# A planner's release time for tiles under an adding transfer, and its wait between small vector instructions, in a two-layer decoder kernel

## The chip, the cores and the metric

The kernel runs on one core of a Trainium2 chip. Its metric is the device time of one execution in microseconds (us). The engines are TensorE (PE, with its weight loads as PEld), VectorE (DVE), ScalarE (ACT), GpSimd (POOL) and SyncE (SP, which here only issues transfers).

## What is computed

The reference is a trunk of two layers on 512 tokens of width 1024, in 32-bit floats:

```python
# per layer (DEPTH = 2, SEQ = 512, D_MODEL = 1024, D_FF = 4096)
xn = rms_norm(h, g_mix);  proj = xn @ w_in
att = dsa_attention(...)        # 8 heads; an indexer keeps the top 128 keys of each query
hm  = sigmoid(m_o) * rms_norm(mlstm_chunkwise(...))      # 4 heads of 128
h = h + concat([att, hm]) @ w_out
u = rms_norm(h, g_mlp) @ w_ff1
h = h + square(relu(u)) @ w_ff2
gate = sigmoid(rms_norm(h, g_ple) @ w_ple_gate + b)
h = h + gate * (p_i @ w_ple)
```

## The kernel before, in words

Every large product is made of three passes over operands split in two: a weight tile `raw` of 128 x 1024 floats comes from memory, ACT writes `hi`, its rounded form, and `lo` holds the rest; the product is hi*hi + hi*lo + lo*hi. There are two ways to get `lo` (`weight`, L521). In the plain way DVE subtracts `hi` from `raw`. In the other ("adder") ACT writes the negative of the rounded form into `lo`, and a transfer issued by POOL adds `raw` to it in place (L533, L534); so `raw` is read by that transfer until it lands. 126 of 212 weight tiles go this way: those of the values, the convolution's projections, the output projection, the second product of the MLP (ff2), and some of the first (ff1) and of the gate.

The rest of ff1 goes by a Strassen scheme (`left` L762, `pair` L792). A pair takes two weight tiles, r1 and r2, and makes sums of their quarters on DVE in `at` and in place; ACT and DVE then split these. In the MLP of a layer seven rounds run; each has two pairs and eight blocks of ff2 (four adder tiles).

Nothing runs in the order in which the program is written. The whole kernel is first recorded as a list of operations with their tiles. `Plan.schedule` (L248) then plays them through by a list of assumed costs: each engine takes the ready operation of highest rank whose new tiles have free places (rank: the longest path to the end, plus an urgency of its label, L51). Places are few: 3 for `raw`, 4 for `hi`, 4 for `lo` (L1341), handed out in the order in which they came free. The order in which each engine took its operations is then its program; the chip keeps it strictly. On the chip true dependencies and reuse of places are guarded by semaphores, so that the planner's times decide order and places, and nothing else.

Three assumed times matter here. `cost` gives a vector instruction on four columns 69 + 4 x 1.042 ns = 73 ns (L229). `lag` (L232) says how long after an operation's end its readers may start: 110 ns from DVE to DVE, and 5,500 ns after an adder was issued. A tile's place comes free `HOP` = 200 ns after the end of the operation that finishes last among its users (L356 to L360); an adder ends, for this purpose, 1,100 ns after POOL takes it.

Chains of small vector instructions stand where a root is taken: `rsqrt` (L545) is ten dependent instructions on tiles of 4 to 16 columns (rooms `tiny` and `wide`), and `spread` (L610) follows with a copy, a difference and two wide products, which TensorE needs to spread the roots over partitions. Between the two stand the first blocks of ff1 in the MLP. `norm`, their label, has an urgency of 180, well above the MLP's 0. On TensorE the matmuls of `mlp` are chained in program order (L189), the spread's two among them.

Of the kernel before, what the change touches and what calls it, by code (L numbers as in the profile page):

```python
# [55 lines left out]
class View:  # L56


    def __init__(self, buf, steps, index, p):
        self.buf, self.steps, self.index, self.p = buf, steps, index, p  # L60
# [66 lines left out]
class Plan:  # L127
# [5 lines left out]
    ENGINES = ("vector", "scalar", "gpsimd", "tensor", "sync")  # L133
    HOP = 200.0

    def __init__(self, rooms, caps):
        self.ops, self.rooms, self.caps = [], rooms, caps
        for e in self.ENGINES:
            setattr(self, e, Engine(self, e))
        self.chain, self.tail, self.hold = None, {}, None  # L140
        self.bufs = 0
        self.label, self.stage, self.bias = None, 0, 0
# [88 lines left out]
    @staticmethod  # L231
    def lag(a, b):  # L232

        if a == "adder":
            return 5500.0
        if a == b:
            return {"vector": 110.0, "scalar": 60.0, "gpsimd": 100.0}.get(a, 0.0)
        if b == "sync":
            return 1220.0
        if a == "sync":  # L240
            return 2200.0
        return 320.0 if b == "tensor" else 200.0 if a == "tensor" else 150.0
# [5 lines left out]
    def schedule(self):  # L248
        ops = self.ops
        for op in ops:  # L250
            for a in op.after:
                ops[a].before.append(op.n)
        for op in reversed(ops):
            c = min(self.cost(f) for f in op.forms)
            op.rank = c + max((ops[b].rank + self.lag(self.source(op), ops[b].forms[0][0]) for b in op.before),
                              default=0.0)
            op.left, op.ready, op.start = len(op.after), 0.0, None
        for op in ops:
            op.rank += 1000.0 * (URGENT.get(op.label, 0) + op.bias) - 1e7 * op.stage
        free = {k: list(range(n)) for k, n in self.rooms.items()}  # L260
        held = dict.fromkeys(self.caps, 0)
        queues = {e: {} for e in self.ENGINES}
        busy = dict.fromkeys(self.ENGINES, False)
        events, now, done = [], 0.0, 0
        live = {}
        idle = [-1e9, 0.0]

        def push(op):
            key = tuple(sorted(b.kind for b in op.new))
            for e in {f[0] for f in op.forms}:  # L270
                heapq.heappush(queues[e].setdefault(key, []), (-op.rank, op.n))

        def fits(op, relaxed=False):
            need = {}
            for b in op.new:
                need[b.room] = need.get(b.room, 0) + 1
            for k, n in need.items():
                if k not in free:
                    continue
                if len(free[k]) < n + (0 if relaxed else (MARGIN.get(op.label, MARGIN["s"]) if k == "s" else MARGIN.get(op.new[0].kind, 0))):  # L280
                    return False
            for b in op.new:
                for group, (kinds, cap) in self.caps.items():
                    if b.kind in kinds and held[group] >= cap:
                        return False
            return True

        for op in ops:
            if not op.left:
                push(op)  # L290
        order = []
        while done < len(ops):
            moved, relaxed = True, False
            while moved or not (events or relaxed):
                relaxed = not moved
                moved = False
                for e in self.ENGINES:
                    if busy[e]:
                        continue
                    best = None  # L300
                    for key, q in queues[e].items():
                        while q and ops[q[0][1]].start is not None:
                            heapq.heappop(q)
                        if q and (best is None or q[0] < best[0]):
                            op = ops[q[0][1]]
                            if fits(op, relaxed):
                                best = (q[0], q)
                    if best is None:
                        continue
                    op = ops[heapq.heappop(best[1])[1]]  # L310
                    op.form = next(f for f in op.forms if f[0] == e)
                    op.start = op.begin = now
                    for b in op.new:
                        live[b.name] = (b, op.label, round(now / 1000))
                        if b.room in free:
                            b.place = free[b.room].pop(0)
                        for group, (kinds, cap) in self.caps.items():
                            if b.kind in kinds:
                                held[group] += 1
                    busy[e] = True  # L320
                    order.append(op)
                    op.end = now + self.cost(op.form)
                    if e == "sync" and not now:
                        op.end += 900.0
                    if e == "tensor":
                        if now - idle[0] > 3300.0:
                            idle[1] = now + 3600.0
                        if now < idle[1]:
                            op.end += self.cost(op.form)
                        idle[0] = op.end  # L330
                    heapq.heappush(events, (op.end, 0, op.n, e))
                    moved = True
                    if relaxed:
                        break
            if not events:
                stuck = [(o.n, o.label, [b.kind for b in o.new]) for e in self.ENGINES for q in queues[e].values()
                         for _, i in q[:3] for o in (ops[i],) if o.start is None]
                self.live = live
                self.stuck = []
                raise RuntimeError(f"no place: {done} of {len(ops)} {stuck[:20]} { {k: len(v) for k, v in free.items()} } {held}")  # L340
            now, what, n, e = heapq.heappop(events)
            op = ops[n]
            if what == 0:
                busy[e] = False
                done += 1
                for b in op.before:
                    o = ops[b]
                    o.ready = max(o.ready, now + self.lag("adder" if op.form[:2] == ("gpsimd", "dma_start") else e,
                                                          o.forms[0][0]))
                    o.left -= 1  # L350
                    if not o.left:
                        if o.ready <= now:
                            push(o)
                        else:
                            heapq.heappush(events, (o.ready, 1, o.n, None))
                for b in {id(v.buf): v.buf for v in op.reads + op.writes}.values():  # L356
                    b.users -= 1
                    if not b.users:
                        heapq.heappush(events, (now + self.HOP, 2, n, b.name))
                        self.gone[b.name] = b  # L360
            elif what == 1:
                push(op)
            else:
                b = self.gone.pop(e)
                live.pop(b.name)
                if b.room in free:
                    free[b.room].append(b.place)
                for group, (kinds, cap) in self.caps.items():
                    if b.kind in kinds:
                        held[group] -= 1  # L370
        self.order, self.span = order, now
# [1055 lines left out]
```

## Time and profile before

| | us |
|---|---|
| median of 3 runs | 1380.51 (1380.43 to 1382.61) |
| profiled execution | 1384.69 |
| its span, first to last instruction | 1383.0 |
| PE busy | 1322.4 (96%) |
| DVE busy | 922.1 (67%) |
| ACT busy | 791.1 (57%) |

The stages of the profiled execution, by its windows: layer 1 has its mixing part to about 240 us, the way into the MLP to 300, the MLP to about 620, the gate to about 665; layer 2 the same from there, with the way into the MLP from 920 to 980 and the MLP to about 1310. All instructions have one line, L390, since the plan issues them in one place; so they are told apart by their tiles: `raw`, `hi`, `lo`, `at` as above, `tiny` and `wide` for the chains, `s` for slots of 128 x 512, `const` for the residual h, `ps_proj` and `ps_tr` for accumulators. Names carry no numbers of places.

### The profile page before, as it was taken

The numbers are of one execution on the slowest core, as the hardware profiler recorded it, in microseconds if no ns is written. First come the engines' busy times: TensorE is split into PE (matmuls) and PEld (weight loads), VectorE is DVE, ScalarE is ACT, GpSimd is POOL, SyncE is SP. The second block draws the span as 40 slices with busy tenths as digits, with TensorE's granted clock in tenths as the row PEclk, the third lists the DMA queues.
The fourth block names the chain that finished last, engine by engine and source line by source line (L and its number), as shares of the span: only waits on it lengthen the run. The fifth ranks groups of instructions, "written<-read, shape, count | busy, mean of one in ns | idle before, by whom it ended". The sixth has DMA issues, their size and how long they took to land. (4 is left out here: it accounts for less than half of the span.)

```text
span 1383.0 us, 20108 instructions
## 1 busy us (share of the span) xinstructions
PE 1322.4 (96%) x7376; PEld 1130.2 (82%) x7376; DVE 922.1 (67%) x2048; ACT 791.1 (57%) x1477; POOL 207.6 (15%) x241
## 2 busy tenths in 40 slices
PE   6999999989999989999999999999899999998998
PEld 6877898778888978888887778987788888887887
DVE  7899886666565646464859998848656464655445
ACT  4886584664444535456548957838554453454552
POOL 4131100310000000004112211003000000100130
PEclk9999999999999999999999999999999999999999
DMA  5556802655655554566335576136465645555761
GB/s 187 130 119 164 198 17 54 161 122 137 155 134 154 134 156 127 147 159 161 106 102 122 132 171 155 32 77 136 130 159 135 156 123 152 138 122 131 193 163 63
DMA packets 53092, 183.73 MB, mean 133 GB/s; under 512 B 6272, under 2 KB 6784, under 8 KB 52992
## 3 DMA queue, kind: packets, MB, share of 16 engines
q1 hardware_dynamic: 34848, 116.37, 26.5%
q0 software_dynamic: 18144, 66.07, 26.1%
q8 instruction: 58, 0.95, 0.3%
q14 instruction: 42, 0.34, 0.1%
HBM read 114.25 MB, written 2.10 MB: 84 GB/s over the span
## 5 line engine op out<-in xcount | busy, mean ns | idle before, releaser
L390 PE MATMUL ps_proj<-s,hi 128*128 128x512 f32 (+1 forms) x3184 | 852.7, 357 | 13.6 <-DVE s L390 11.1
L390 PEld LDWEIGHTS ps_proj<-s,hi 128*128 128x128 f32 x3184 | 560.1, 190 | 106.6 <-DVE s L390 15.1
L390 PE MATMUL ps_proj<-s,lo 128*128 128x512 f32 (+1 forms) x1592 | 563.1, 356 | 3.3 <-DVE lo L390 3.3
L390 ACT ACTIVATE hi<-raw 128x1024 fp32r<-128x1024 f32 (+1 forms) x212 | 221.8, 1049 | 250.7 <-PE ps_proj L390 153.3
L390 PEld LDWEIGHTS ps_proj<-s,lo 128*128 128x128 f32 x1592 | 301.8, 190 | 49.2 <-DVE lo L390 4.4
L390 POOL DMA_DIRECT2D lo<-raw x126 | 108.9, 864 | 973.9 <-ACT lo L390 753.3
L390 DVE TENSOR_TENSOR lo<-raw,hi 128x1024 fp32r<-128x1024 f32 (+1 forms) x85 | 104.9, 1234 | 118.6 <-ACT hi L390 97.3
L390 DVE TENSOR_TENSOR const<-const,ps_proj 128x512 f32<-128x512 f32 x160 | 108.5, 683 | 99.0 <-PE ps_proj L390 98.7
L390 ACT ACTIVATE lo<-raw 128x1024 fp32r<-128x1024 f32 x126 | 132.5, 1052 | 16.6 <-DMA raw<-ws 8.5
L390 PE MATMUL ps_proj<-hi,s 128*128 128x512 f32 (+1 forms) x384 | 112.9, 380 | 8.5 <-ACT hi L390 7.8
L390 DVE TENSOR_TENSOR s<-s,s 128x512 fp32r<-128x512 f32 (+2 forms) x124 | 86.9, 741 | 27.4 <-ACT s L390 27.2
L390 ACT ACTIVATE s<-raw 128x512 fp32r<-128x512 f32 x28 | 17.7, 630 | 144.7 <-DVE raw L390 144.7
L390 ACT ACTIVATE s<-s 128x512 fp32r<-128x512 f32 (+2 forms) x154 | 88.6, 621 | 18.8 <-DMA s<-pt 11.3
L390 PEld LDWEIGHTS ps_proj<-hi,s 128*128 128x128 f32 x384 | 70.0, 193 | 18.9 <-ACT hi L390 7.8
L390 PE MATMUL ps_sc<-s,s 128*128 128x512 f32 (+3 forms) x288 | 83.7, 376 | 0.5 <-ACT s_idx L390 0.2
L390 POOL TENSOR_TENSOR s<-s,s 128x512 f32<-128x512 f32 x42 | 64.2, 1530 | 71.8 <-ACT s L390 63.5
L390 DVE TENSOR_TENSOR at<-raw 128x512 f32<-128x512 f32 x28 | 19.4, 693 | 83.3 <-DMA raw<-ws 83.3
L390 PE MATMUL ps_proj<-lo,s 128*128 128x512 f32 (+1 forms) x192 | 65.8, 382 | 1.7 <-DVE lo L390 1.7
L390 PE MATMUL ps_proj<-s,s 128*128 128x256 f32 x336 | 47.2, 292 | 14.6 <-ACT s L390 14.6
L390 PEld LDWEIGHTS ps_proj<-s,s 128*128 128x128 f32 x336 | 44.7, 196 | 19.9 <-ACT s L390 18.2
L390 PEld LDWEIGHTS ps_sc<-s,s 128*128 128x128 f32 x288 | 50.6, 190 | 10.9 <-issue 2.2
L390 DVE TENSOR_TENSOR s<-s,ps_proj 128x256 f32<-128x256 f32 x84 | 35.0, 417 | 32.6 <-PE ps_proj L390 32.6
(150 smaller groups left out, 1613.3 us busy)
## 6 DMA issues: line engine op xcount, KB each, us to landing
raw<-ws SPq DMA_DIRECT2D x204, 512.0 KB, 4.2
lo<-raw POOLq DMA_DIRECT2D x126, 512.0 KB, 5.6
raw<-wa SPq DMA_DIRECT2D x8, 336.0 KB, 3.4
const<-xt SPq DMA_DIRECT2D x8, 256.0 KB, 5.0
s<-pt SPq DMA_DIRECT2D x8, 256.0 KB, 7.3
out<-const SPq DMA_DIRECT2D x7, 256.0 KB, 2.0
const<-ct SPq DMA_DIRECT2D x2, 132.0 KB, 3.4
out<-const SPq DMA_DIRECT2D x2, 128.0 KB, 1.7
```

What stands on the lines that cost most here:

```text
L390: ins = getattr(getattr(nc, e), method)(*[value(x) for x in args], **{k: value(x) for k, x in kw.items()}).ins
```

## The change

The release of a tile's place and the wait between two vector instructions are planned otherwise; the recorded operations are the same.

```diff
     HOP = 200.0
+    ADD = 5500.0
...
         if a == "adder":
-            return 5500.0
+            return Plan.ADD
...
                 for b in op.before:
                     o = ops[b]
-                    o.ready = max(o.ready, now + self.lag("adder" if op.form[:2] == ("gpsimd", "dma_start") else e,
-                                                          o.forms[0][0]))
+                    wait = self.lag(self.source(op), o.forms[0][0])
+                    if e == o.forms[0][0] == "vector" and o.writes[0].buf.room in ("tiny", "wide"):
+                        wait = 0.0
+                    o.ready = max(o.ready, now + wait)
...
                     b.users -= 1
                     if not b.users:
-                        heapq.heappush(events, (now + self.HOP, 2, n, b.name))
+                        heapq.heappush(events, (now + (self.ADD if self.source(op) == "adder" else self.HOP), 2, n, b.name))
```

`source(op)` is "adder" for a transfer issued by POOL, and otherwise the engine of the operation's first form. A vector operation that waits for a vector operation, and itself writes first into a `tiny` or `wide` tile, may start in the plan as soon as the other ends. The place of a tile comes free 5,500 ns after the end of the operation that was last to finish with it, if that operation is an adder. Ranks are the same as before.

## Rows read from the trace of the kernel before

**Rows 1.** The page's first part: busy us, share of the span, instructions.
```profile
PE 1322.4 (96%) x7376; PEld 1130.2 (82%) x7376; DVE 922.1 (67%) x2048; ACT 791.1 (57%) x1477; POOL 207.6 (15%) x241
```

**Rows 2.** Waits of PE, whole span: waiter, releaser, us in total, times, longest.
```profile
PE ps_proj L390 <- ACT s L390: 15.8, 11, 3.5
PE ps_proj L390 <- DVE s L390: 11.1, 13, 1.9
PE ps_tr L390 <- DVE s L390: 7.1, 4, 3.0
```

**Rows 3.** PE's timeline, 971 to 978: start, us, instruction [idle before, releaser].
```profile
975.72 0.50 PE L390 MATMUL ps_tr<-s,const 128*128 128x512 f32 x1 [2.95 <-DVE s L390]
976.99 0.50 PE L390 MATMUL ps_tr<-s,const 128*128 128x512 f32 x1 [0.77 <-DVE s L390]
```

**Rows 4.** DVE's timeline, 966 to 977.6.
```profile
967.13 0.16 DVE L390 SCALAR_TENSOR_TENSOR tiny<-tiny,tiny 128x4 f32<-128x4 f32 x1
967.33 0.16 DVE L390 SCALAR_TENSOR_TENSOR tiny<-tiny 128x4 f32<-128x4 f32 x1
968.67 1.23 DVE L390 TENSOR_TENSOR lo<-raw,hi 128x1024 fp32r<-128x1024 f32 x1 [1.18 <-ACT hi L390]
...
972.92 0.69 DVE L390 TENSOR_TENSOR at<-raw 128x512 f32<-128x512 f32 x1 [2.95 <-DMA raw<-ws]
...
974.98 0.68 DVE L390 TENSOR_TENSOR s<-const,tiny 128x512 fp32r<-128x512 f32 x1
...
976.25 0.68 DVE L390 TENSOR_TENSOR s<-const,tiny 128x512 fp32r<-128x512 f32 x1
```

**Rows 5.** The chain that ended last, 955 to 978: start, us, what.
```profile
963.94 5.32 DMA lo<-raw
969.32 3.58 DMA raw<-ws
```

**Rows 6.** Waits of PE in layer 2's MLP, 980 to 1310.
```profile
PE ps_proj L390 <- ACT s L390: 7.4, 5, 2.1
PE ps_proj L390 <- DVE s L390: 5.9, 5, 1.9
```

**Rows 7.** The chain that ended last, 1071 to 1104.
```profile
1089.64 6.79 DMA lo<-raw
...
1096.49 5.76 DMA raw<-ws
```

**Rows 8.** ACT's timeline, 1084 to 1104.
```profile
1087.77 0.63 ACT L390 ACTIVATE s<-raw 128x512 fp32r<-128x512 f32 x1 [8.58 <-DVE raw L390]
1088.31 1.04 ACT L390 ACTIVATE lo<-raw 128x1024 fp32r<-128x1024 f32 x1
...
1090.20 1.05 ACT L390 ACTIVATE hi<-raw 128x1024 fp32r<-128x1024 f32 x1
```

**Rows 9.** POOL's timeline, 1088 to 1097.5.
```profile
1089.64 0.86 POOL L390 DMA_DIRECT2D lo<-raw  x1 [15.38 <-ACT lo L390]
```

**Rows 10.** Waits of SP's queue, whole span.
```profile
SPq L390 <- DMA lo<-raw: 838.4, 119, 41.0
```

**Rows 11.** DVE's instructions on tile `tiny` by stretch: us, busy (count), clock, DMA, GB/s.
```profile
40.00:80.00 40.00, 11.00 (x56) 1.00 0.56 130
80.00:180.00 100.00, 2.33 (x25) 0.98 0.68 163
...
980.00:1300.00 320.00, 0.00 (x0) 0.99 0.56 140
```

**Rows 12.** DVE's timeline, 24.9 to 30.5, where two chains alternate.
```profile
25.62 0.16 DVE L390 TENSOR_TENSOR tiny<-tiny,tiny 128x4 f32<-128x4 f32 x1
25.72 0.19 DVE L390 SCALAR_TENSOR_TENSOR wide<-wide,wide 128x32 f32<-128x32 f32 x1
25.83 0.16 DVE L390 SCALAR_TENSOR_TENSOR tiny<-tiny,tiny 128x4 f32<-128x4 f32 x1
```

**Rows 13.** All engines, 80 to 180: us, PE, PEld, DVE, ACT, POOL busy.
```profile
80.00:180.00 100.00, 97.26 (x457) 77.20 (x456) 93.55 (x266) 70.03 (x154) 19.17 (x31) 0.98 0.68 163
```

## The prediction, made before the changed kernel was run

> **What bounds the kernel now.** I read the page's busy times first. TensorE is busy for 1322.4 of 1383.0 us [rows 1], so 60.6 us is the most that any order of the same instructions could give back, and some of it (the start before the first weights, the end after the last matmul) is not in question. Then the waits of TensorE over the whole span [rows 2]: it waited 15.8 us for ScalarE's instructions on slots, 11.1 for VectorE's, and 7.1 us, in only four waits, between a matmul into `ps_tr` and VectorE. The reader is to see that these are single waits of 1 to 3.5 us, not a steady shortage. Then the places. The `ps_tr` waits stand on the way into each MLP: 2.95 and 0.77 us in layer 2 [rows 3], and the other two of the four, 7.1 less 3.72, make 3.4 us in layer 1. About half of the waits for ScalarE stand in layer 2's MLP, 7.4 us, with 5.9 for VectorE [rows 6]. These two kinds have different causes, and the two halves of the change aim at one each.
>
> **The chain on the way into the MLP.** VectorE's own timeline shows the cause [rows 4]. Members of the root's chain follow each other at 967.33 - 967.13 = 0.20 us. After 967.33 three more small instructions stand before the first wide product (the last two of the root, the copy). Run through, that product would begin at 967.33 + 4 x 0.20 = 968.1. It began at 974.98, because the plan's 110 ns let other instructions in between: the split of r1 at 968.67 with 1.18 us of waiting before it, and `at<-raw` at 972.92 with 2.95, held until r2 had landed. That landing was itself late, behind an adder of 5.32 us and a load of 3.58 [rows 5]. VectorE keeps its order, so TensorE waited for a weight that the chain doesn't use.
>
> With the wait at nothing and an urgency of 180, in the plan the chain's next member is ready at the moment VectorE comes free, and outranks all of the MLP; the copy, the difference and both wide products follow, for their producers write `tiny` tiles. On the chip: the first product from 968.1 to 968.8, the difference at 0.20, the second by 969.7. TensorE came to the spread at 975.72 - 2.95 = 972.77 [rows 3], 3 us after that. All four waits go: -7.1 us [rows 2]. r1's split moves from 968.67 to 969.7 and is over by 970.9, still ahead of r2's landing at 972.9, so it costs nothing. If that cover were gone (r2 landing 2 us earlier), r2's sums would start up to 1 us later, before products that stand a whole round of matmuls ahead. Late next is r2 itself: its sums run on its landing as before.
>
> **Does the gain stay?** Loads of `raw` are paced by places, and those by TensorE's progress and by adders. TensorE 3.6 us ahead in each MLP may meet the next late load: from 0 to all 3.6 given back per layer, up to 7.1 in all. The first round behind the spread has no wait of TensorE in the trace, so I take 0.5 us for both.
>
> **The held tile.** The release reads the operation that ends last among a tile's users. It is an adder only if `hi` was made before the adder's issue ended. In the MLP the order is mostly the other way. An example: POOL takes an adder at 1089.64 for 0.86 us [rows 9], while ScalarE makes that tile's `hi` from 1090.20 to 1091.25 [rows 8]. There the tile is still released 200 ns after ScalarE, as before, and the change does nothing. I went through the timelines of ScalarE and POOL for all 126 adders: `hi` ends later in 59 of the 72 in both MLPs and in 22 of the other 54. So 45 tiles are held 5.3 us longer in the plan: output projections, most of the convolution, the gate, the first and last of each MLP. On the chip that hold is nothing new: SP already waited 838.4 us for adders to land, 119 times [rows 10], with no other duty in most of them. The planned load moves later and stays where it was on the chip. Its price lies between -14 us (if it did reorder the MLP as in the first rival) and, on the other side, 13 such tiles in the MLPs at the nearest wait, 2.95 us [rows 3], = +38, if each held a load too long. I take 0: the nearest row is the wait that SP has already.
>
> [...]
>
> **Chains elsewhere.** The MLP's rounds hold no instruction on `tiny` at all; 40 to 80 us holds 56 and 80 to 180 holds 25 [rows 11]. In alternation two chains go at (25.83 - 25.62) / 2 = 0.105 us an instruction [rows 12], run through at 0.20. Where VectorE is full, 93.55 of 100 us [rows 13], 25 such instructions would cost up to 25 x 0.095 = 2.4 us of VectorE in each layer. TensorE beside it is at 97.26 and has other work, so little reaches it. On the other side chains that end earlier could remove small waits. Taking the waits for slots [rows 2] less those that stand in both MLPs and on the way into them bounds this near 5 us. From -5 to +5, I take +1, nearer to the full VectorE.
>
> [...]
>
> **Sum.** -7.1 + 0.5 + 0 + 1.0 = -5.6 us. The profiled execution took 1384.69, 1.7 us over its span and 4.2 over the median of the runs; on it that gives 1379.1. The waits that go are set by the order, not by that run, so I take the same 5.6 from the median: 1380.5 - 5.6 = 1374.9, rounded 1375.
>
> **Rivals.** *The hold reaches the MLP after all.* The waits in the MLPs come from r2's late landing and from adders: ScalarE was idle 8.58 us before `s<-raw` and only then made the `lo` whose adder took 6.79 us; the next r1 load waited for that and took 5.76 [rows 7, 8]. If the plan knew, the `lo` would be ordered ahead of it. For it: the 13 held tiles and an earlier spread shift the start of each MLP, and an order can turn on that. Against it: 59 of 72 tiles are released as before. Of twice (7.4 + 5.9) = 26.6 us [rows 6] about half would go: 5.6 + 13 gives 1362.
>
> *The plan becomes too hopeful.* The planner now counts 73 ns for a link of a chain (before, 183), where the chip takes 0.20 us [rows 4]. A chain of 12 ends 1.5 us later than planned, and TensorE, which keeps its order, waits wherever the plan put a dependent matmul right behind. For it: the mixing parts are full of such chains (query root, key norms, gates, four heads' normalisers), about 9 in a layer. Against it: TensorE has ready work ahead of most, and is at 97.26 of 100 [rows 13]. All 18 would cost 27 us, half of them 13.5: with -7.1 that is +6.4, 1387. It decides from about five such waits on, where it has eaten the gain.
>
> *Given back.* The next late load in each MLP takes the 3.6 us again, because loads and adders pace it [rows 7], not the spread. Then 1380.5 + 1 = 1381, no change that can be measured. That the change doesn't do what it says is in this sum already, for the held tile.
>
> **How the numbers follow.** The forecast has 0.55, with its own range 1370 to 1379; the hold reaching the MLP 0.14; given back 0.17; the hopeful plan 0.14. 0.2% is 2.8 us, about what a measurement of this kernel can tell from no change: faster is below 1377.7, slower above 1383.3. Faster: 0.9 of the forecast's and the first rival's, 0.50 + 0.14 = 0.64. Within: the rest of the forecast's and most of the given back, 0.05 + 0.15 = 0.20. Slower: the hopeful plan and the tail of the given back, 0.16. The range of 8 in 10 runs from 1363, which leaves out half of the first rival, to 1387, which leaves out the worse half of the third and some 2 in 100 of the rest.
>
> **What would show it.** The waits of TensorE for `ps_tr` by VectorE should fall from 7.1 to under 1 us, and VectorE's timeline on the way into each MLP should show the root, the copy and the first wide product unbroken at 0.20 us. The waits in the MLPs should stay near 7.4 and 5.9 us in layer 2, with `at<-raw` still waiting for r2; if they fall by half, the first rival is right. Waits of TensorE in 40 to 240 and 720 to 920 that grow by more than 5 us, behind `tiny` tiles, would show the second. If the four waits go and the MLPs last 3 us longer, it is the third. A total above 1383 with the four waits gone would make the prediction wrong in its sum; the four waits unchanged would make it wrong in its mechanism.

## The result: 0.6% slower, and where the time went

The changed kernel took 1389.3 us (median of 12 runs, 1383.9 to 1396.7), the kernel before 1381.1 (12 runs beside them, 1378.8 to 1385.9): a ratio of 1.0062, with a 95% interval of 1.0042 to 1.0083, or about 8.6 us more. Its profiled execution took 1389.29, with a span of 1387.6.

The page after, first line (busy us, share, instructions; [rows 1] before): the same work to within 4 us on TensorE, 13.5 more on VectorE.

```profile
PE 1318.4 (95%) x7376; PEld 1128.6 (81%) x7376; DVE 935.6 (67%) x2047; ACT 791.3 (57%) x1478; POOL 205.0 (15%) x241
```

TensorE's waits over the whole span after (releaser: us, times, longest); [rows 2] before:

```profile
PE ps_proj L395 <- ACT s L395: 19.6, 11, 3.2
PE ps_proj L395 <- DVE s L395: 9.9, 9, 2.5
...
PE ps_tr L395 <- DVE s_hn L395: 4.1, 3, 1.6
PE ps_tr L395 <- DVE tiny L395: 2.8, 4, 1.1
PE ps_tr L395 <- DVE s L395: 2.2, 2, 1.4
...
PE ps_sc L395 <- DVE tiny L395: 1.8, 2, 0.9
...
PE ps_sc L395 <- DVE s L395: 1.4, 1, 1.4
```

The 7.1 us for `ps_tr` on the way into the MLPs are gone (the two `ps_tr` waits left on VectorE's `s` stand elsewhere). New are waits of the mixing part: for `s_hn`, for `tiny`, and of score matmuls (`ps_sc`). By stretch the sums of all waits, before and after, are: the two mixing parts 7.5 and 18.0, the ways into the MLPs 11.3 and 4.4, the MLPs 25.0 and 28.0, the rest 11.3 and 13.5. In all 55.1 became 63.9.

The four waits went as the prediction said. VectorE's timeline on the way into layer 2's MLP, after ([rows 4] before):

```profile
976.35 0.17 DVE L395 CAST tiny<-tiny 128x4 fp32r<-128x4 f32 x1
976.55 0.16 DVE L395 TENSOR_TENSOR tiny<-tiny,tiny 128x4 f32<-128x4 f32 x1
976.63 1.28 DVE L395 TENSOR_TENSOR s<-const,tiny 128x512 fp32r<-128x512 f32 x2
977.83 1.22 DVE L395 TENSOR_TENSOR lo<-raw,hi 128x1024 fp32r<-128x1024 f32 x1
981.33 0.69 DVE L395 TENSOR_TENSOR at<-raw 128x512 f32<-128x512 f32 x1 [2.27 <-DMA raw<-ws]
```

Both wide products now stand behind the last link and ahead of r1's split, and `at<-raw` waits for r2 as before, with nothing of the chain behind it. The loss is elsewhere. TensorE's waits in 720 to 920, first the kernel before, then the one after:

```profile
PE ps_tr L390 <- ACT s_kh L390: 1.2, 1, 1.2
PE ps_proj L390 <- ACT s L390: 0.9, 2, 0.6
PE ps_proj L390 <- DVE s L390: 0.3, 1, 0.3
PE ps_pn L390 <- ACT s_hn L390: 0.2, 1, 0.2
```

```profile
PE ps_tr L395 <- DVE s_hn L395: 2.5, 2, 1.4
PE ps_sc L395 <- DVE s L395: 1.4, 1, 1.4
PE ps_tr L395 <- ACT s_kh L395: 1.2, 1, 1.2
PE ps_up L395 <- DVE lo L395: 1.1, 1, 1.1
PE ps_proj L395 <- ACT s L395: 1.0, 1, 1.0
PE ps_sc L395 <- DVE tiny L395: 0.9, 1, 0.9
PE ps_tr L395 <- ACT s L395: 0.7, 1, 0.7
PE ps_tr L395 <- DVE tiny L395: 0.7, 1, 0.7
```

Eight waits of 0.86 to 1.55 us, four in each mixing part, make 9.8 us; each stands behind one unbroken chain of the mLSTM's normaliser. One of them, on VectorE before and after (the same kind of stretch, about 3 us of it):

```profile
186.39 0.15 DVE L390 TENSOR_TENSOR tiny<-tiny,tiny 128x4 f32<-128x4 f32 x1
186.46 0.42 DVE L390 CUSTOM_DVE_ANT_0 s_e<-ps_sc,s 128x256 f32<-128x256 f32 x1
...
186.81 0.17 DVE L390 RECIPROCAL tiny<-tiny 128x4 f32<-128x4 f32 x1
186.97 0.56 DVE L390 CUSTOM_DVE_ANT_0 s_e<-ps_sc,s 128x384 f32<-128x384 f32 x1
...
188.18 0.15 DVE L390 SCALAR_TENSOR_TENSOR tiny<-tiny,tiny 128x4 f32<-128x4 f32 x1
188.37 0.17 DVE L390 TENSOR_SCALAR tiny<-tiny 128x4 f32<-128x4 f32 x1
188.45 0.55 DVE L390 CUSTOM_DVE_ANT_0 s_e<-ps_sc,s 128x384 f32<-128x384 f32 x1
```

```profile
186.36 0.15 DVE L395 SCALAR_TENSOR_TENSOR tiny<-tiny,tiny 128x4 f32<-128x4 f32 x1
186.54 0.37 DVE L395 TENSOR_SCALAR tiny<-tiny 128x4 f32<-128x4 f32 x2
...
188.53 0.16 DVE L395 SCALAR_TENSOR_TENSOR tiny<-tiny,tiny 128x4 f32<-128x4 f32 x1
188.72 0.16 DVE L395 TENSOR_TENSOR tiny<-tiny,tiny 128x4 f32<-128x4 f32 x1
188.80 0.42 DVE L395 CUSTOM_DVE_ANT_0 s_e<-ps_sc,s 128x256 f32<-128x256 f32 x1
```

and TensorE's timeline at its end, after:

```profile
189.28 0.44 PE L395 MATMUL ps_tr<-const,s_e 128*128 128x128 f32 x2 [1.14 <-DVE tiny L395]
```

Before, the attention's `s_e` stood between the links, and TensorE went on. After, 13 links run from 186.36 to 188.88, the next `s_e` starts at 188.80, and TensorE, which ran nothing from 188.14 on, waits 1.14 us for it. (The trace names `tiny` here for the accumulator read that closes this `s_e`, at 189.14, not for a link.) In five of the eight waits it is such work of others behind the chain that TensorE waits for, in three it is the chain's own result, `s_hn`. VectorE is not short of time there. The windows of 180 to 250, before and after (us, then busy us and count of PE, PEld, DVE, ACT, POOL, then clock, transfers):

```profile
180.00:250.00 70.00, 69.35 (x476) 61.61 (x474) 47.96 (x165) 41.71 (x124) 4.33 (x7) 1.00 0.21 48
```

```profile
180.00:250.00 70.00, 65.95 (x467) 59.34 (x468) 49.34 (x169) 42.20 (x134) 3.58 (x6) 1.00 0.16 36
```

VectorE is busy for 48 or 49 of 70 us in both; TensorE loses 3.4.

### The profile page after: what moved, and what is told of

Same layout as the page of the kernel before. It is cut to its first block, busy times and chain, and to the rows that moved or that the text cites. A ratio compares the mean times of both kernels' runs of the same rounds, so it can differ in the third digit from the quotient of the medians.

```text
span 1387.6 us, 20092 instructions
## 1 busy us (share of the span) xinstructions
PE 1318.4 (95%) x7376; PEld 1128.6 (81%) x7376; DVE 935.6 (67%) x2047; ACT 791.3 (57%) x1478; POOL 205.0 (15%) x241
## 5 line engine op out<-in xcount | busy, mean ns | idle before, releaser
L395 PEld LDWEIGHTS ps_proj<-s,hi 128*128 128x128 f32 x3184 | 559.6, 190 | 100.9 <-DVE s L395 13.4
L395 PE MATMUL ps_sc<-s,s 128*128 128x256 f32 (+3 forms) x288 | 82.5, 373 | 3.2 <-DVE tiny L395 1.8
L395 POOL TENSOR_TENSOR s<-s,s 128x512 f32<-128x512 f32 x42 | 60.9, 1449 | 73.3 <-ACT s L395 63.8
L395 PE MATMUL ps_proj<-s,s 128*128 128x256 f32 x336 | 47.5, 293 | 18.6 <-ACT s L395 18.6
L395 ACT ACTIVATE s<-ps_tr 128x128 fp32r<-128x128 f32 (+2 forms) x174 | 42.6, 319 | 29.4 <-PE ps_tr L395 28.9
```

Of the source, the lines that this page charges most:

```text
L395: ins = getattr(getattr(nc, e), method)(*[value(x) for x in args], **{k: value(x) for k, x in kw.items()}).ins
```

## The experiments

Two things had to be told apart besides the parts of the change. A new plan is a new order for most of the kernel (in the changed kernel some 1650 of the 1888 planned vector operations have another position), and may be better or worse by itself. And in before's trace TensorE's granted clock is at 0.50 of full speed nine times, for 3.4 us each (once 6.8, and the last 2.5 us of the span), which loses 16.6 us; seven of the nine begin within 2.4 us of the end of a wait of 0.8 to 3.5 us (one from 977.7 to 981.1, right behind the waits of [rows 3]). The clock's mean differs between executions of one kernel (before: 0.984 to 0.996). In all 20 traces here the span, less TensorE's waits, less span x (1 - granted clock), is 1308 to 1316 us. So I subtract that last product from each timed run, and call the rest "outside the clock's losses"; it varies by 1 to 3 us (standard deviation) between runs of one kernel. Before lost 13 to 16 us to the clock on average. For the runs of before beside the changed kernel the clock is not on record; its "about +6" takes the other sets of before.

All runs; differences are of means, to the runs of before on the same chip; the waits are those of TensorE in both mixing parts, from the profiled execution (before: 7.5); they depend by about 1 us, in after_lag by 2, on where a stage is taken to end.

| kernel | ratio to before (95%) | us | outside the clock | waits |
|---|---|---|---|---|
| the change | 1.0062 (1.0042, 1.0083) | +8.6 | about +6 | 18.0 |
| hold_only | 1.0065 (1.0043, 1.0086) | +7.9 | +2.5 | 11.2 |
| run_only | 1.0140 (1.0110, 1.0170) | +18.6 | +14.9 | 23.9 |
| run_norm | 0.9990 (0.9970, 1.0011) | -1.6 | +0.3 | 7.8 |
| run_mlstm | 1.0101 (1.0072, 1.0130) | +13.1 | +7.6 | 16.2 |
| but_mlstm | 1.0033 (1.0014, 1.0052) | +4.7 | +1.4 | 12.1 |
| null_lag | 1.0124 (1.0085, 1.0164) | +16.9 | +4.6 | 15.3 |
| null_hop | 0.9943 (0.9922, 0.9965) | -8.6 | -6.7 | 7.0 |
| after_hop | 1.0003 (0.9984, 1.0022) | +0.6 | +3.9 | 17.8 |
| hold_hop | 0.9950 (0.9931, 0.9969) | -7.7 | -4.6 | 10.4 |
| norm_hop | 0.9896 (0.9866, 0.9926) | -13.4 | -5.3 | 7.3 |
| mlstm_hop | 1.0079 (1.0050, 1.0109) | +9.3 | +5.8 | 18.3 |
| but_mlstm_hop | 0.9974 (0.9959, 0.9990) | -3.5 | -3.1 | 12.5 |
| after_lag | 1.0281 (1.0243, 1.0319) | +39.9 | +24.4 | 35.6 |
| pull_mlstm | 1.0244 (1.0214, 1.0273) | +33.4 | +16.1 | 23.0 |
| pull_norm | 0.9998 (0.9977, 1.0019) | -0.1 | -0.2 | 7.1 |
| pull_spread | 0.9978 (0.9953, 1.0004) | -3.1 | +0.2 | 6.9 |
| run_priced | 1.0032 (1.0010, 1.0053) | +4.5 | +1.4 | 15.0 |
| null_priced | 1.0146 (1.0108, 1.0183) | +18.5 | +9.0 | 15.2 |

The theories that the expectations name: **A**, small chains of the mLSTM run through on VectorE while TensorE waits for the attention's vector work; **B**, the new order alone, as before's was a good draw; **C**, the held tiles cost time; **D**, what is gained on the way into the MLP is given back at the next late load.

### The two halves, and two labels alone

*hold_only*: the release of the change, and no chain run through.

```diff
-                    if e == o.forms[0][0] == "vector" and o.writes[0].buf.room in ("tiny", "wide"):
+                    if False:
```

> Of the change only the later release of tiles whose last user is an adder; vector chains wait 110 ns in the plan as before. Theory A (the time was lost to the mLSTM's small chains, run through on VectorE while TensorE waits for attention's vector work): within 2 us of the kernel before, the four waits of TensorE for ps_tr by VectorE on the way into the MLPs still there, 7 us. Rival B (any new order of this many instructions loses a few us against an order that happened to be good, whatever moved it): 4 to 8 us slower. Rival C (the held tiles cost the time): about 8 us slower.

*run_only*: chains run through, the release as before.

```diff
-heapq.heappush(events, (now + (self.ADD if self.source(op) == "adder" else self.HOP), 2, n, b.name))
+heapq.heappush(events, (now + self.HOP, 2, n, b.name))
```

> Of the change only the chains of small vector instructions that run through; tiles are released as before. Theory A: the whole loss, 6 to 10 us slower than before, with waits of 0.9 to 1.6 us behind the mLSTM's chains (about 178, 188, 196, 219 us and the same in layer 2). Rival B: 4 to 8 us slower, but without those waits being the sum. Rival C: no slower than before, or faster by the 7 us of the waits on the way into the MLPs.

*run_norm* and *run_mlstm*: run_only, for the readers of one label alone (`norm`: the roots on the way into an MLP and at the start of a layer; `mlstm`: the four heads' normalisers).

```diff
-                    if e == o.forms[0][0] == "vector" and o.writes[0].buf.room in ("tiny", "wide"):
+                    if e == o.forms[0][0] == "vector" and o.writes[0].buf.room in ("tiny", "wide") and o.label == "norm":
```

> Chains run through only where the reader has the label norm (the root of the token norms and its spread); tiles are released as before. The planned order is nearly that of before: few instructions move. Theory A: 5 to 7 us faster than before (1374 to 1376), the four ps_tr waits gone, the mixing parts as before. Rival B: no loss, since little moves, and the same gain or less. Rival D (the time gained on the way into an MLP is given back at its next late load): within 2 us of before, with the MLP's waits longer by what the four waits were.

> Chains run through only where the reader has the label mlstm; tiles are released as before. Theory A: 8 to 11 us slower than before, with about eight new waits of TensorE of 0.9 to 1.6 us (9.8 us in the changed kernel) where a chain of 13 runs for 2.5 us, and the ps_tr waits on the way into the MLPs unchanged at 7 us. Rival B: 4 to 8 us slower with waits spread anywhere. Rival C: as before.

Measured: run_mlstm alone is 13.1 us slower, with eight new waits of 0.87 to 1.60 us, and run_only 18.6: theory A's place and kind, and more than the 8 to 11 and 6 to 10 us that it gave. hold_only is 7.9 us slower, as B and C had it and not A; but only 2.5 of that lie outside the clock's losses, which could be the new order as well as the hold. run_norm gains nothing, though its `ps_tr` waits are gone. TensorE's timeline there, once in each layer, right behind the first round of the MLP:

```profile
305.22 0.50 PE L395 MATMUL ps_proj<-s,hi 128*128 128x256 f32 x2 [2.61 <-DVE s L395]
```

```profile
983.16 0.71 PE L395 MATMUL ps_proj<-s,hi 128*128 128x256 f32 x2 [2.36 <-DVE s L395]
```

Those are new, 5.0 us together. The waits on the ways into the MLPs fell from 11.3 to 4.2 us, those in the MLPs rose from 25.0 to 32.0, and all its waits sum to 56.5 us, against 55.1 before: D. Its order is nearly that of before (95 vector operations have another position).

### Without a new plan: pull_mlstm, pull_norm, pull_spread

Here the order of before is kept on every engine, and afterwards VectorE's small links alone are moved (the cut below is pull_mlstm's; pull_spread moves the two wide products as well).

```diff
+        def emit(op):
+            emitted.add(op.n)
+            pulled.append(op)
+            for i in sorted(op.before):
+                o = ops[i]
+                if i in emitted or o.label not in ('mlstm',) or o.form[0] != "vector" or not chained(o) or not chained(op):
+                    continue
+                if all(a in emitted for a in o.after):
...
+                    emit(o)
```

> The order of before on every engine, with one thing done to it afterwards: on VectorE the members of the mLSTM's chains that write tiny or wide tiles are pulled together behind their first member (170 instructions move, all else keeps its place; nothing is planned anew). Theory A: the cost of running these chains through without a new plan, +8 to +10 us, 1389 to 1392, with TensorE waits of about 1 to 1.5 us behind chains of 2.5 us in both mixing parts. Theory B: hardly anything is reordered, so 0 to 2 us, 1380 to 1384.

> The order of before on every engine, with one thing done to it afterwards: on VectorE the members of the norm's chains that write tiny or wide tiles are pulled together behind their first member (66 instructions move, nothing is planned anew). The prediction's own step alone: 1375, -6 to -7, with the ps_tr waits on the way into the MLPs gone and the MLPs no longer. Theory D (given back at the next late load): the ps_tr waits shrink or go, and as much comes back right behind the spread or in the MLP, 1379 to 1384.

> The order of before, with the norm's links pulled together as in pull_norm and, in addition, the two products on the way into each MLP that TensorE waits for (s<-const,tiny) moved behind the last link (70 VectorE instructions move, nothing else, nothing is planned anew). This is the prediction's first term by itself. The prediction: the ps_tr waits before the MLPs (8.1 us with their ps_proj companions) go and stay gone, 1375 to 1378. D: they go and come back as waits for VectorE's or ScalarE's s right behind the spread, since r2's sums and the copies still run when r2 has landed, 1380 to 1384.

pull_mlstm lost 33.4 us, far more than A expected, 16.1 of it outside the clock. Moving 170 of some 1890 vector operations did that. TensorE's timeline, and the windows around it (the last three columns are granted clock, share of the transfers, GB/s):

```profile
190.79 0.56 PE L418 MATMUL ps_tr<-const,s_e 128*128 128x128 f32 x2 [2.56 <-DVE tiny L418]
```

```profile
180.00:190.00 10.00, 8.23 (x69) 7.79 (x68) 8.60 (x41) 8.32 (x36) 0.88 (x3) 1.00 0.01 2
190.00:195.00 5.00, 4.21 (x23) 4.22 (x24) 3.19 (x12) 2.40 (x8) 0.00 (x0) 0.66 0.00 0
195.00:203.00 8.00, 7.90 (x70) 7.58 (x68) 5.51 (x24) 6.07 (x26) 0.00 (x0) 1.00 0.00 0
203.00:212.00 9.00, 6.99 (x31) 6.40 (x32) 5.03 (x19) 3.18 (x8) 0.00 (x0) 0.62 0.01 2
```

The reader is to see both halves of the loss: the wait of 2.56 us, and behind it a stretch whose granted clock is 0.66 of full speed, 1.7 us lost in those 5. The same follows the next chain's wait, of 2.12 us, before 205.01 (3.4 us lost in 203 to 212). The mechanism of A needs no new plan, then. run_mlstm, which was planned with its chains, lost 13.1; that a plan adapts to some of it would explain the difference, and is not shown.

pull_norm changed nothing, and its trace says why:

```profile
975.19 0.80 PE L418 MATMUL ps_tr<-s,const 128*128 128x512 f32 x1 [2.99 <-DVE s L418]
```

The links were together, but the wide products that TensorE waits for write `s`, and stayed behind r2's sums. pull_spread moves these too, and is the prediction's first term by itself. Its `ps_tr` waits are gone, and one of 1.6 or 1.7 us in each layer comes behind the first round. TensorE, ScalarE and VectorE in layer 2:

```profile
976.46 0.50 PE L441 MATMUL ps_proj<-s,hi 128*128 128x256 f32 x2 [1.68 <-DVE s L441]
```

```profile
973.70 1.05 ACT L441 ACTIVATE hi<-raw 128x1024 fp32r<-128x1024 f32 x1
974.65 1.04 ACT L441 ACTIVATE lo<-raw 128x1024 fp32r<-128x1024 f32 x1
975.59 0.36 ACT L441 ACTIVATE s<-ps_proj 128x256 f32<-128x256 f32 x1
```

```profile
975.99 0.42 DVE L441 TENSOR_TENSOR s<-s,ps_proj 128x256 f32<-128x256 f32 x1 [0.79 <-ACT s L441]
```

ScalarE makes a `hi` and a `lo` before it copies the accumulator, VectorE waits for that copy, TensorE for VectorE's sum. TensorE's order is that of before, so that its waits can be set side by side matmul by matmul: those on the ways into the MLPs fell from 11.3 to 4.2 us, the whole 7.1; those in the MLPs rose from 25.0 to 28.2, by the two behind the first rounds; 1.5 more came in the first 40 us; and all of them went from 55.1 to 52.2. The time fell by 3.1 of the 7.1 us predicted, with an interval that includes no change, and outside the clock's losses by nothing. The result lies between the two expectations, D's mechanism in the trace, in about half its full size.

The same holds in all kernels here. In the ten whose norm's chains are together with the two products behind them (the changed one, after_hop, after_lag, but_mlstm, but_mlstm_hop, norm_hop, run_norm, run_only, run_priced, pull_spread), no wait for these products is left, and a new one of 0.8 to 2.6 us stands behind the first round of the MLP in 19 of 20 layers. In the other ten the waits for the products are there, 2.1 to 4.8 us in a layer, and none stands behind the first round.

### Two controls, and the same change on other plans

*null_lag* and *null_hop* have nothing of the change; one planned figure is moved by a tenth.

```diff
-            return {"vector": 110.0, "scalar": 60.0, "gpsimd": 100.0}.get(a, 0.0)
+            return {"vector": 120.0, "scalar": 60.0, "gpsimd": 100.0}.get(a, 0.0)
```

```diff
-    HOP = 200.0
+    HOP = 220.0
```

> The kernel before with one planned figure moved a little: the lag from a VectorE instruction to its VectorE reader is 120 ns instead of 110. No tile is held longer and no chain runs through; the order of most VectorE instructions changes all the same. A control. By theory A (the loss is TensorE waiting behind normaliser chains of the mLSTM that run unbroken) nothing is lost: 1380 to 1385, TensorE's waits in 40 to 240 and 720 to 920 stay near 5 and 3 us. By theory B (the order of before is a lucky one, and any reordering loses some us) it is 4 to 8 us slower, 1385 to 1390, as hold_only was.

> The second control: the kernel before with the planned hop between two engines, and with it the release of a tile, at 220 ns instead of 200. A: 1380 to 1385. B: 4 to 8 us slower. If both controls lie within 2 us of before, the 9 us of hold_only need another cause than its being a reordering; if both lie 5 or more above, they need none.

One lost 16.9 us, the other gained 8.6: neither theory expected that. A new plan alone moves the time by as much as the whole effect in question or more, and before's order is no special one. So the change was put on both of these plans (*after_hop*, *after_lag*: the figure above in the changed kernel), and its parts on the better one (*hold_hop*, *mlstm_hop*, and *norm_hop*, which is null_hop with run_norm's line).

> The whole change (hold and chains) on a plan whose hop between engines is 220 ns instead of 200; its before is null_hop, which took 1374.0. Theory A (the change itself costs): above null_hop by 5 to 15, 1379 to 1389, with TensorE's waits of 0.9 to 1.6 us behind unbroken mLSTM chains again in both mixing parts. Theory B (each new plan is a draw, the change no more than that): as likely below 1374 as above, anywhere from 1366 to 1390, and the waits of the mixing parts not behind those chains.

> The whole change on a plan whose VectorE lag is 120 ns instead of 110; its before is null_lag, which took 1396.9. A: above it, 1400 to 1410, or, if null_lag already pays for the same kind of wait (it has one of 4.57 us at 170 and one of 2.24 at 235 in the mixing part), about equal, 1394 to 1400, with waits behind the mLSTM chains. B: back towards the middle of all plans, 1375 to 1392.

> null_hop with the norm's chains run through and no others, nothing held longer: the part of the change that did no harm on the plan that was best. A and D: the ps_tr waits before the MLPs (4 to 5.5 us a layer in null_hop) fall to about 2, part of it is given back in the MLP: 1368 to 1375. B: anywhere from 1366 to 1390.

> null_hop (the plan with a hop of 220 ns, 1374.0) with the mLSTM's chains run through and no others, nothing held. A: most of what after_hop lost against null_hop (10.6 us outside the clock's losses): 1381 to 1387, TensorE's waits in the mixing parts 6 to 12 us above null_hop's 7.0. B: a draw, as likely below 1374 as above.

> null_hop with the held tiles and no chain run through. If holding costs by itself (theory C; hold_only was +2.8 us outside the clock's losses on the other plan), 1377 to 1384; if hold_only's loss was the draw of a new order, anywhere from 1366 to 1390 and no new kind of wait, and TensorE's waits outside the mixing parts unchanged within 2 us.

The change costs on all three plans: +8.6, +9.2 (0.6 less -8.6) and +23.0 (39.9 less 16.9). That is against B as the whole cause, though B's scatter is real, and three draws would all fall on the slow side one time in eight. after_hop and norm_hop lie where A had them, mlstm_hop (median 1390.6) and after_lag (1423.1) above. On the plan with the longer hop its parts, against null_hop, are: the mLSTM's chains +17.9, the hold +0.9, the norm's chains -4.8. The last compares two sets of runs, and outside the clock's losses it is +1.4, so it is no gain that is shown. The hold (C) is +2.5 and +2.1 us outside the clock on the two plans, and +7.9 and +0.9 with it, no more than a new plan gives.

### The whole change without the mLSTM's chains

*but_mlstm* and *but_mlstm_hop*: the whole change, at the two hops.

```diff
-                    if e == o.forms[0][0] == "vector" and o.writes[0].buf.room in ("tiny", "wide"):
+                    if e == o.forms[0][0] == "vector" and o.writes[0].buf.room in ("tiny", "wide") and o.label != "mlstm":
```

> The whole change (hold, chains run through, hop 200) except that the mLSTM's chains keep the 110 ns. If they make the loss, it goes: TensorE's waits in the mixing parts fall from 18.0 (after) to about 8 or less, outside the clock's losses 4 to 8 us below after (1374.5), 1378 to 1386 in all. If chains run through anywhere cost alike (the indexer's, the first part's), the loss stays within 2 us of after.

> The same on the plan with a hop of 220: the whole change except in the mLSTM's chains. If these make the loss, it lies 6 to 12 us below after_hop and near null_hop and norm_hop, 1370 to 1378, which is below before. If not, it stays near after_hop, 1381 to 1388.

Both came out lower than the whole change, by 3.9 us (8.6 less 4.7) and 4.1 (0.6 less -3.5); outside the clock's losses by some 4.5 and 7.0, which is most of what the change costs there (about 6 and 10.6). The waits in the mixing parts fell from 18.0 to 12.1 and from 17.8 to 12.5, not to 8. In layer 2's each has one wait for `s_hn` that before has not, of 2.9 and 3.1 us, at 909 and 901, so that the mLSTM's chains are not the whole of it.

### The plan's price

*run_priced* is run_only with the price that the chip shows (links at 0.20 us), *null_priced* the same price without running through.

```diff
-                    op.end = now + self.cost(op.form)
+                    op.end = now + max(self.cost(op.form), 200.0 if e == "vector" and op.writes[0].buf.room in ("tiny", "wide") else 0.0)
```

> Chains run through everywhere (no longer hold), but the plan charges at least 200 ns for each VectorE instruction that writes a tiny or wide tile, which is the pace at which the chip was seen to run them. If the loss comes from the plan's wrong price (it thinks a chain of 13 over 1.5 us early and puts the dependent matmul right behind), it goes: within 2 us of before or better, 1378 to 1384, and TensorE's waits in the two mixing parts fall back to about 8 us in all from 18. If the unbroken chain itself is the cause (2.5 us in which VectorE serves nobody else, whatever the plan knows of it), it stays 6 to 12 slower, 1387 to 1394, with the waits behind the chains still 1 to 1.5 us each.

> The control for run_priced: the plan charges 200 ns for each small VectorE instruction, and chains do not run through. If running through costs by itself even at the right price, it lies below run_priced, at 1375 to 1383; if at the right price it costs nothing, the two agree within 4 us, 1383 to 1391, and the whole loss of run_only (15 us above run_priced) was the price.

With the price that the chip shows for a link, run through costs 14.1 us less than at 73 ns (4.5 against 18.6), and 14.0 less than not run through at the same price. Neither kernel came out as expected: run_priced, at 1387.6, lies between its two branches, with waits of 15.0 us in the mixing parts and not 8, and null_priced, at +18.5, fits neither of its own.

The planner's own total says more. It is the time at which `Plan.schedule`, run on a kernel's file, ends (`span` in the code); for before it is 1228.7 us, some 150 below the chip's, so that only differences to before are compared. null_lag's plan is 17.6 us longer and null_priced's 18.0, and the chip measured 16.9 and 18.5: these two were slower plans, and not poor draws. null_hop's is 1.6 shorter, measured 8.6. The six kernels that run the mLSTM's chains through at 73 ns lie 6.4 to 21.1 us above what their plans promise (the changed one: planned -5.1, measured +8.6). The other ten new plans lie between 12.2 below and 2.2 above, and run_priced, with its chains run through at 200 ns, is one of them: planned +5.5, measured +4.5. So the plan fails where the mLSTM's chains are run through and priced too low. One plan with the right price is few, though, and pull_mlstm shows that unbroken chains also cost where the order was never planned for them. That running through is free, or even of use, in a plan that prices it rightly is likely by this and not shown.

## Why the prediction was wrong, point by point

- **The four waits go, -7.1.** Right, in place and size: 11.3 us on the ways into the MLPs became 4.4, by the steps worked out (both products behind the last link, r1's split still over before r2 lands: 979.05 against 981.33). One reason in it is wrong. The products don't follow because "their producers write `tiny` tiles": the edit asks what the reader writes, and they write `s`. They keep the 110 ns, of which the difference covers 73, and in the plan nothing else was ready for VectorE in the rest. And the sum lacks what stood beside the four waits: in before's trace the clock is at 0.50 right at their ends, from 295.0 to 301.8 and from 977.7 to 981.1, which loses 5.1 us. The timed runs of pull_spread lost 11.0 us to the clock on average, those of before beside them 14.3, and its gain of 3.1 us lies all in that.
- **Does the gain stay, 0.5 given back.** Mis-sized. The waits in both MLPs rose by 3.0 us in the changed kernel, by 3.2 in pull_spread and by 7.0 in run_norm; of the time, with the term alone, 3.1 of 7.1 stayed in pull_spread and 1.6 in run_norm, neither clear of zero. The step of this term that failed is "the first round behind the spread has no wait of TensorE in the trace": it had none because TensorE came to it late. ScalarE's splits and r2's sums, which run on landings, were just on time for the late TensorE, and are late for the early one (1.68 us in layer 2 of pull_spread).
- **The held tile, 0.** Not refuted, and not shown: +7.9 us and +0.9 on the two plans, 2.5 and 2.1 of it outside the clock, where hold_only's own plan is 6.4 longer. SP's waits for adders fell, from 838.4 us [rows 10] to 789.9.
- **Chains elsewhere, +1.** This is the step that failed and turned the sign. It measured +10.5 us of waits in the mixing parts, 9.8 of them the eight behind the mLSTM's chains. Two faults stand in it. It read the stretch of 80 to 180, where VectorE is full [rows 13], and so asked what VectorE's time is worth; the chains that hurt stand at 175 to 222 and 873 to 913, where VectorE was idle, before, for 6.2 of 47 and 8.5 of 40 us. And it took TensorE's 97 of 100 us as cover, though TensorE keeps its order too and stood idle for 1.14 us behind the chain that ended at 188.88: the matmul there was due, not spare. Its other bound was too wide as well: the waits for slots, 34.0 us [rows 2], less 20.8 in both MLPs (13.3 [rows 6] and 7.5 in layer 1, which the first rival took at 13.3 too) and 11.3 on the ways, leave 1.9 us to gain, not 5.
- **The rival "the plan becomes too hopeful"**, held at 0.14, is what the trace shows: TensorE waits behind chains that the plan prices at 73 ns a link, eight times (it had set five as the point of decision), for 0.86 to 1.55 us (it had 1.5). That the price makes these waits is likely by the planned totals above; what it did not have is that the matmul need not depend on the chain, as five of the eight don't. Its forecast of 1387 was at the upper bound of the range. The profile could have raised it: before, those chains stood interleaved with `s_e`, one link at a time, at just the places where TensorE had no wait.
- **What no step had:** that a new plan alone moves the time (8.6 us down, 16.9 and 18.5 up in three controls, the last two as planned), and that behind a wait of 1 to 3 us the clock can be at half as well (1.7 us lost behind 2.56 in pull_mlstm).

What stays open: how much of the 8.6 us is this plan's draw. Without the mLSTM's chains some 4.5 of about 6 us outside the clock's losses go, and 7.0 of 10.6 at the longer hop, each time in a new plan, which can itself move the time by as much. The rest of the 8.6, some 3 us by difference, is the clock's, and was not settled.

The fastest kernel here is norm_hop, at 0.9896 of before (0.9866 to 0.9926), median 1372.45, and it beats both kernels. Most of that it shares with null_hop (0.9943), from which only the norm's chains tell it apart, so it is a good order, not an argument for the edit.

## What to carry to other kernels

When engines keep a planned order, a chain of small dependent instructions is best run through only where nobody waits for what stands behind it (here TensorE did, eight times, for 9.8 us); look, at each place where it will run unbroken, at what the engine would have served in between, and not at how busy the engine is. A planner's price for a dependent link has to be the pace at which the chip runs it (here 0.20 us, and 73 ns in the plan), or every reader is put too early. And before an edit of a planner is credited or blamed, move one of its figures a little without the edit: if that moves the time as much, judge the edit on several plans, or on a fixed order, and set each measured difference beside the one that the planner itself gives.

## What was not expected of the hardware

Behind single waits of TensorE its granted clock was lower, a loss on top of the wait. In pull_mlstm it was 1.00 from 180 to 190, and 0.66 and 0.62 in the stretches around and behind the ends of waits of 2.56 and 2.12 us for VectorE (190 to 195 and 203 to 212), so that some 1.7 and 3.4 us were lost beside them. It is not so behind every wait: the eight of the changed kernel, 0.86 to 1.55 us long, left the clock at 1.00, and so did one of 2.08 us in before, which ended at 1037.3. That the waits are the cause is not shown. Over the timed runs the mean loss to the clock went from 8.2 us (norm_hop) to 31.8 (after_lag), only roughly in the order of the kernels' waits.

Links of 4 columns, each dependent on the one before, followed at 0.20 us (13 from 186.36 to 188.88 in the changed kernel, 2.52 us) though each is shown with 0.15 to 0.17; two chains in alternation, one of 4 columns and one of 32, took VectorE 0.105 us a link in before [rows 12].
